# Attention stage of a hybrid decoder step: queries and keys whole in fp32 with two heads in the array's row halves, a values product with queries in partitions, and sample scores four batches at a time

## The chip, the cores and the metric

The kernel runs on one core of a Trainium2 chip. The metric is the device time of one execution in microseconds (us). Engines are named as in the profile: PE is TensorE's matrix multiplication, PEld its weight load, DVE is VectorE, ACT ScalarE, POOL GpSimd, SP SyncE.

## What is computed

One step of a one-layer decoder with 512 prompt tokens and a group of 8 samples of 4 tokens each (32 rows), which share the weights. The two paths read one combined projection:

```python
h = rmsnorm(x, g) * (1 + mods[1]) + mods[0]
q, kc, vc, kv_sel, kv_win, gates, z, xbc, dt = in_proj(h, w_in, g_q, g_k_sel, g_k_win)
# attention: 8 query heads, 2 key-value heads, head size 64
s = jnp.einsum('btgqd,bmgd->btgqm', q, k) * SCALE      # SCALE = 64 ** -0.5
p = masked_softmax(s, mask)
o = jnp.einsum('btgqm,bmgd->btgqd', p, v)
o = gates[:, :, 0] * o_cmp + gates[:, :, 1] * o_sel + gates[:, :, 2] * o_win
# state-space path: causal conv on x/B/C, chunked scan, gate and norm
x = x + mods[2] * (concat(rmsnorm(o), y_ssm) @ w_out)
x = x + mods[5] * hier_moe(rmsnorm(x, g2) * (1 + mods[4]) + mods[3], ...)
```

Attention has three branches: compressed blocks of 32 tokens, selected blocks of 64, and a window of 512. For the prompt the window covers all 512 tokens and at most 8 blocks exist, so its selected and window branches are both causal attention, with different keys and values. The samples have a past of 2048 tokens in paged caches; their selected branch ranks 32 blocks and gathers pages, and their window branch reads a cache of 512 rows.

## The kernel before

Tokens of the prompt lie in four tiles of 128 (`t` = 0 to 3). The program has four stages, each with its own set of PSUM tiles: modulation weights, projections with the prompt's state-space chunks, the attention stage (from `open_psum("pp2", ...)`, L768), and the out projection with the expert part (MoE).

The order of instructions on each engine is not the order of the source alone: a scheduler sets it when the program is built, from data dependencies, buffers and priorities, and it mixes independent pieces. So what stands beside what has to be read from the built order.

In the attention stage the prompt's two causal branches are eight calls `attend(t, br)`, `br` = 1 for the window (`wino` holds keys and values) and 0 for the selected branch (`selo`). Queries `QT` and keys `KT` are kept transposed and in fp32r, a 32-bit form that PE takes in one pass, as a high part and the rest: each head's 64 query columns are split into high and rest over 128 rows (L903 to L915, tile `qhl`), and keys stand twice, once for each half (`k_stack`, L775 to L791, tile `khl`). One head's scores are then two matmuls on 128 rows, and a third adds the causal mask `negm` on the diagonal block (L806 to L813). DVE reduces the row maximum (L815, `amx`), ACT takes the exponential (L817, `psb`), PE transposes it (L820, `pt`), an evacuation (`evac`, L100 on DVE or L102 on ACT) copies it to `ptsb`, and the values product writes `ot` with head columns in partitions, two heads in the two column halves of the array:

```python
mm(ot[64 * i:64 * i + 64, h2 * P:(h2 + 1) * P], src[:, c, P + g * 64:P + (g + 1) * 64],
   pts[i][:, c * P:(c + 1) * P], start=c == 0, stop=c == t)
```

Here the values (64 columns) are stationary and 128 queries move. At the end `ot` is copied (`ots`, L829), transposed back in four transposes (L836), scaled by gate and sum on DVE (L838), and added into `att` on POOL (L841). Score tiles `s` have two buffers of one bank.

The samples' work runs between these calls: `win_half` and `sel_first`/`sel_second` for two halves of four batches. Each transposes gathered keys (`kt<-sm`, L1023), multiplies them by the block-diagonal queries `Qb` (`smo<-kt,Qb`: a 32-column block per batch, 512 columns), and takes a softmax and a values product (`smo<-gsel,kt`). Before that DVE norms and scales the sample rows (L854 to L872) and ranks the blocks (L1201 to L1205). The samples' state-space chain (L1244 to L1348: conv `xcS`, states `hst`, decay `dcS`, sums L1340) and the prompt's compressed attention (L1355 to L1420) are also in this stage. The next stage begins with the transposes of `zy` (L1521), which need the PSUM tiles of the attention stage.

All matmuls are issued by the helper at L92. An fp32 matmul shows as two records of the profile, an fp32r or bf16 one as one.

Of the kernel before, what the change touches and what calls it, by code (L numbers as in the profile page):

```python
# [9 lines left out]
F32 = mybir.dt.float32  # L10
F32R = mybir.dt.float32r
# [39 lines left out]
def hybrid_step(ctx: ExitStack, tc: tile.TileContext, a, o):  # L51
# [501 lines left out]
    V.tensor_scalar_mul(gq8, gq, SCALE)  # L553

# [195 lines left out]

    steps = dict(C=proj_c, z=proj_z, p=ssd_prep, q=proj_q, B=proj_b, e=ssd_end)
# [16 lines left out]
    open_psum("pp2", s=2, pt=2, ot=1, sm=2, smo=1)  # L768
# [3 lines left out]
    QT = p2.tile([P, 8, 512], F32R, name="QT")  # L772
    KT = p2.tile([P, 2, 2, 2, 512], F32R, name="KT")

    def k_stack(src, br):  # L775
        kq = W(p2, [P, NT, P], F32, "t512", 2)
        V.tensor_tensor(kq.rearrange("p t (g d) -> p t g d", d=64),
                        src[:, :, 0:P].rearrange("p t (g d) -> p t g d", d=64),
                        gq8[:, None, None, :].to_broadcast([P, NT, 2, 64]), op=OP.mult)
        kq4 = kq.rearrange("p t (g d) -> p (t g) d", d=64)[:, :, None, :].to_broadcast([P, NT * 2, 2, 64])  # L780
        khl = SLOT([P, 2, NT * 2, 2, 64], F32R, "khl")
        V.tensor_copy(khl[:, 0], kq4)
        V.tensor_sub(khl[:, 1], kq4, khl[:, 0].bitcast(F32))
        for g in range(2):
            for hl in range(2):
                x = khl[:, hl]
                ps = PS("s")
                for t in range(NT):
                    T.transpose(ps[:, t * P:(t + 1) * P],
                                x[:, 2 * t + g].rearrange("p a d -> p (a d)").bitcast(F32), ident)  # L790
                evac(KT[:, br, g, hl, :], ps)  # L791


# [6 lines left out]
    def attend(t, br, first=False):  # L800
# [4 lines left out]
        for h2 in range(4):  # L805
            pts = []  # L806
            for h in (2 * h2, 2 * h2 + 1):
                g = h // 4
                ps = PS("s")
                q = QT[:, h, t * P:(t + 1) * P]  # L810
                mm(ps[:, 0:n], q, KT[:, br, g, 0, 0:n], start=True, stop=False)
                mm(ps[:, 0:n], q, KT[:, br, g, 1, 0:n], start=False, stop=False)
                mm(ps[:, t * P:n], identb, negm, start=False, stop=True)  # L813
                mx = W(p2, [P, 1], F32, "amx", 4)
                V.tensor_reduce(mx, ps[:, 0:n], axis=AX.X, op=OP.max, negate=True)  # L815
                pb = W(p2, [P, 512], F32, "psb", 3)
                S.activation(pb[:, 0:n], ps[:, 0:n], AF.Exp, bias=mx, accum_out=sm[:, h:h + 1])  # L817
# [3 lines left out]
                pts_sb = W(p2, [P, 512], F32, "ptsb", 3)  # L821
                evac(pts_sb[:, 0:n], pt[:, 0:n])
                pts.append(pts_sb)
            g = h2 // 2
            for c in range(t + 1):
                for i in range(2):
                    mm(ot[64 * i:64 * i + 64, h2 * P:(h2 + 1) * P], src[:, c, P + g * 64:P + (g + 1) * 64],
                       pts[i][:, c * P:(c + 1) * P], start=c == 0, stop=c == t)
        ots = W(p2, [P, 512], F32, "psb", 3)  # L829
        evac(ots, ot)  # L830
# [3 lines left out]
        po = PS("s")  # L834
        for h2 in range(4):
            T.transpose(po[:, h2 * P:(h2 + 1) * P], ots[:, h2 * P:(h2 + 1) * P], ident)  # L836
        tmp = att[:, t, :] if first else W(p2, [P, 512], F32, "t512", 2)
        V.tensor_tensor(tmp.rearrange("p (h d) -> p h d", d=64), po.rearrange("p (h d) -> p h d", d=64),  # L838
                        sm[:, :, None].to_broadcast([P, 8, 64]), op=OP.mult)
        if not first:  # L840
            G.tensor_add(att[:, t, :], att[:, t, :], tmp)  # L841
# [61 lines left out]
    for t in range(NT):  # L903
        qn3 = qa[:, t, :].rearrange("p (h d) -> p h d", d=64)
        if t % 2 == 0:
            qhl = SLOT([P, 2, 8, 2, 64], F32R, "qhl")
        q2 = qhl[:, t % 2]
        S.copy(q2[:, :, 0, :], qn3)
        V.tensor_sub(q2[:, :, 1, :], qn3, q2[:, :, 0, :].bitcast(F32))
        for hf in range(2):  # L910
            ps = PS("s")
            for h in range(4):
                T.transpose(ps[:, h * P:(h + 1) * P], q2[:, 4 * hf + h].rearrange("p a d -> p (a d)").bitcast(F32),
                            ident)
            evac(QT[:, 4 * hf:4 * hf + 4, t * P:(t + 1) * P], ps.rearrange("p (h c) -> p h c", c=P))  # L915


    pi = C3([P, 1], I32, "pi3")
    G.iota(pi, pattern=[[0, 1]], base=0, channel_multiplier=1)
    io8 = C3([P, 8], F32, "io8")  # L920
    G.iota(io8, pattern=[[1, 8]], base=0, channel_multiplier=0, allow_small_or_imprecise_dtypes=True)
    ia = C3([P, 1], I32, "ia")
    ib = C3([P, 1], I32, "ib")
    tf = C3([P, 1], F32, "tf")
    gqf = C3([P, 1], F32, "gqf")
    V.tensor_scalar(ia, pi, 2, 3, op0=OP.logical_shift_right, op1=OP.bitwise_and)
    V.tensor_copy(tf, ia)
# [1248 lines left out]
```

## Time and profile before

| | us |
|---|---|
| median of 3 runs | 783.35 (783.32 to 785.89) |
| the profiled execution | 787.62 |
| its span, first to last instruction | 785.9 |
| attention stage, first query transpose to first `zy` transpose | 258.45 to 489.19 |

The profile comes from one execution, the 787.62 one. The span is what the trace shows; 1.7 us lie around it. Durations of matmuls are modelled and overlap their neighbours in a pipeline, so the distance between two starts says more than one duration. A clock of 1.0 is TensorE's upper level, 2.4 GHz, and 0.5 the lower, 1.2 GHz.

### The profile page before, as it was taken

To read this page: it belongs to the slowest core of one execution; us is meant where nothing else is said; L and a number is where in the kernel's file an instruction comes from. 1 tells how busy PE (TensorE), PEld (TensorE's weight loads), DVE (VectorE), ACT (ScalarE), POOL (GpSimd) and SP (SyncE) were. 2 spreads that over 40 slices of the span, in tenths; PEclk is the share of its full clock that TensorE was granted. 3 is DMA by queue.
4 is the path that set the end of the run, shared out by engine and by line. 5 is a ranking of instruction groups with operands and counts; after the bars stand their busy time and mean duration, and the time that the engine had idled before them with its cause. 6 is when DMAs were issued, how large, how long until landed. Compare 5 with 4: busy or idle time off the path is not lost. (4 is left out here: it accounts for less than half of the span.)

```text
span 785.9 us, 14689 instructions
## 1 busy us (share of the span) xinstructions
PE 709.3 (90%) x5565; PEld 511.7 (65%) x5565; DVE 501.2 (64%) x1333; ACT 355.2 (45%) x813; POOL 151.6 (19%) x169
## 2 busy tenths in 40 slices
PE   4999999898999578998989999899668999999993
PEld 3667877676777355665647756687655766767562
DVE  5633692524644767554557555878986888877773
ACT  3423444515233333364434435613433766677661
POOL 1103012121321421010111200020131232233221
PEclk9999999889899879699999889999868999999997
DMA  8964895144559634423445041988767899997311
GB/s 286 355 187 131 289 330 193 58 162 161 214 191 346 253 143 172 149 81 134 164 158 219 2 108 23 360 267 286 290 253 282 270 333 335 334 329 256 86 25 23
DMA packets 67094, 161.86 MB, mean 206 GB/s; under 512 B 19005, under 2 KB 31238, under 8 KB 60622
## 3 DMA queue, kind: packets, MB, share of 16 engines
q1 hardware_dynamic: 56798, 115.54, 42.3%
q0 software_dynamic: 10224, 45.37, 17.5%
q8 instruction: 44, 0.72, 0.4%
q14 instruction: 28, 0.23, 0.1%
HBM read 153.48 MB, written 20.74 MB: 222 GB/s over the span
## 5 line engine op out<-in xcount | busy, mean ns | idle before, releaser
L92 PE MATMUL acc<-wh,hH 128*128 128x512 f32 (+1 forms) x128 | 48.9, 382 | 0.5 <-issue 0.5
L92 PE MATMUL acc<-wl,hH 128*128 128x512 f32 (+1 forms) x128 | 47.3, 370 | 0.0
L92 PE MATMUL acc<-wh,hL 128*128 128x512 f32 (+1 forms) x128 | 47.1, 368 | 0.0
L817 ACT ACTIVATE psb<-s,amx 128x128 f32<-128x128 f32 (+3 forms) x64 | 33.7, 528 | 27.4 <-DVE amx L815 24.3
L92 PE MATMUL acc<-gu,XF 128*128 128x512 f32 x88 | 46.1, 606 | 0.0
L92 PE MATMUL acc<-wh,XH 128*128 128x512 f32 x68 | 44.7, 657 | 0.4 <-ACT XH L1942 0.4
L815 DVE TENSOR_REDUCE amx<-s 128x1 f32<-128x128 f32 (+3 forms) x64 | 30.9, 484 | 17.3 <-PE s L92 17.3
L92 PE MATMUL ps<-wada,scT 128*32 128x128 f32 x768 | 38.0, 301 | 4.1 <-DMA wada<-in_w_ada 3.0
L92 PE MATMUL s<-KT,QT 128*128 128x384 f32 (+3 forms) x128 | 39.3, 392 | 1.3 <-DVE qa L838 0.8
L335 DVE TENSOR_TENSOR wl<-dn,wh 128x512 fp32r<-128x512 f32 x52 | 34.0, 686 | 7.0 <-ACT wh L334 6.9
L92 PEld LDWEIGHTS ps<-wada,scT 128*32 128x32 f32 x768 | 30.6, 122 | 10.3 <-issue 3.6
L1047 POOL DMA_INDIRECT gsel<-in_cache_sel,idx x16 | 20.6, 1289 | 84.3 <-PE smo L92 72.6
L334 ACT CAST wh<-dn 128x512 fp32r<-128x512 f32 x52 | 30.9, 619 | 12.9 <-PE acc L92 11.2
L820 PE MATMUL pt<-ident,psb 128*128 128x128 f32 x160 | 33.3, 308 | 3.3 <-ACT psb L817 3.3
L1991 POOL DMA_INDIRECT out_y_prompt<-yo,gi x13 | 21.4, 1646 | 74.8 <-DVE yo L1985 20.1
L335 DVE TENSOR_TENSOR wl<-gu,wh 128x512 fp32r<-128x512 f32 x44 | 29.5, 685 | 8.4 <-ACT wh L334 7.6
L92 PE MATMUL acc<-wh,HH 128*128 128x512 f32 x68 | 32.3, 478 | 1.6 <-ACT HH L1974 1.2
L334 ACT CAST wh<-gu 128x512 fp32r<-128x512 f32 x44 | 26.1, 619 | 15.8 <-PE acc L92 10.8
L92 PE MATMUL smo<-kt,Qb 128*32 128x512 f32 x80 | 29.6, 614 | 2.3 <-DVE kt L100 2.3
L102 ACT COPY kt<-sm 128x512 f32<-128x512 f32 x32 | 18.5, 584 | 27.6 <-PE sm L1023 24.0
L1985 DVE TENSOR_TENSOR yo<-acc,M 128x512 f32<-128x512 f32 x34 | 23.1, 686 | 11.5 <-PE acc L92 9.1
L92 PE MATMUL acc<-wl,HH 128*128 128x512 f32 x68 | 28.6, 421 | 0.0
(788 smaller groups left out, 1902.9 us busy)
## 6 DMA issues: line engine op xcount, KB each, us to landing
wada<-in_w_ada SPq DMA_DIRECT2D x24, 1024.0 KB
dn<-in_w_down SPq DMA_DIRECT2D x12, 1024.0 KB
gu<-in_w_gate SPq DMA_DIRECT2D x21, 512.0 KB
gu<-in_w_up SPq DMA_DIRECT2D x21, 512.0 KB
gux<-in_w_gate SPq DMA_DIRECT2D x11, 512.0 KB
gux<-in_w_up SPq DMA_DIRECT2D x11, 512.0 KB
wt<-in_cache_win SPq DMA_DIRECT2D x4, 1024.0 KB
wout<-in_w_out SPq DMA_DIRECT2D x4, 1024.0 KB
```

Source lines behind the costliest of these rows:

```text
L92: T.matmul(out, lhsT, rhs, start=start, stop=stop)
L102: S.copy(out, in_)
L334: S.copy(wh[:, 0:n], w)
L335: (eng or V).tensor_sub(wl[:, 0:n], w, wh[:, 0:n].bitcast(F32))
L815: V.tensor_reduce(mx, ps[:, 0:n], axis=AX.X, op=OP.max, negate=True)
L817: S.activation(pb[:, 0:n], ps[:, 0:n], AF.Exp, bias=mx, accum_out=sm[:, h:h + 1])
L820: T.transpose(pt[:, c * P:(c + 1) * P], pb[:, c * P:(c + 1) * P], ident)
L1047: G.indirect_dma_start(out=t.rearrange("p r c -> p (r c)"), out_offset=None, in_=sel_rows, in_offset=bass.IndirectOffsetOnAxis(ap=idx[:, 2 ...
L1985: V.tensor_tensor(yo[:, cols], po, M5[:, cols], op=OP.mult)
L1991: G.indirect_dma_start(out=y_p, out_offset=bass.IndirectOffsetOnAxis(ap=gi, axis=0), in_=yo, in_offset=None, bounds_check=511, oob_is_err= ...
```

## The change

Queries and keys stay whole in fp32. A tile of 128 rows holds one head of each of the two key-value groups (`q` of group 0 in rows 0 to 63, `q` of group 1 in rows 64 to 127), so one transpose serves two heads, the scale goes onto the keys when ACT copies them out (`k_turn`), and the two heads' scores are matmuls on 64 rows each, in the upper and the lower half of the array. They write a score tile of two banks, of which there is one. For t below 2 one reduction covers both heads. The values product has the transposed weights stationary and 64 value columns moving, so `ot` has queries in partitions; the copy and the four transposes at the end are gone, and the sum into `att` is on DVE. `psb` and `ptsb` have four buffers. The sample scores of four batches are issued by `four_scores`, which ties them to each other in the order 3, 0, 1, 2. Constants and masks are made before the projections, under a lower priority; the window cache tiles have a pool of their own, and the first two gathers are issued early. The source order of the calls is other than before. The compressed scores become four matmuls.

```diff
+    def PS2(tag):
+        return psum["pool"].tile([P, 2, 512], F32, name=nm(tag), tag=tag, bufs=psum["tags"][tag])
...
+    gqc = const([P, 1], F32, "gqc")
+    V.tensor_scalar_mul(gqc, gqr, SCALE)
...
-                S.copy(qa[:, t, :], acc[t])
+                S.copy(qa[:, t, :].rearrange("p (q g d) -> p q g d", q=4, g=2),
+                       acc[t].rearrange("p (g q d) -> p q g d", q=4, g=2))
...
+    with tc.high_priority(offset=-2500):
...
+        PB = CS([P, 2, 8], F32, "PB")
...
-    open_psum("pp2", s=2, pt=2, ot=1, sm=2, smo=1)
+    open_psum("pp2", s=1, pt=2, ot=1, sm=2, smo=1)
...
-    QT = p2.tile([P, 8, 512], F32R, name="QT")
-    KT = p2.tile([P, 2, 2, 2, 512], F32R, name="KT")
-
-    def k_stack(src, br):
...
+    QT = p2.tile([P, 4, 512], F32, name="QT")
+    KT = p2.tile([P, 2, 512], F32, name="KT")
+
+    def k_turn(src, br):
+
+        ps = PS("pt")
+        for t in range(NT):
+            T.transpose(ps[:, t * P:(t + 1) * P], src[:, t, 0:P], ident)
+        S.activation(KT[:, br], ps, AF.Copy, scale=gqc)
...
+        for q in range(4):
+            s2 = PS2("s")
+            for g in range(2):
+                gs = slice(64 * g, 64 * g + 64)
+                mm(s2[:, g, 0:n], QT[gs, q, t * P:n], KT[gs, br, 0:n], start=True, stop=False)
+            for g in range(2):
+                mm(s2[:, g, t * P:n], identb, negm, start=False, stop=True)
+            mx = W(p2, [P, 2], F32, "amx", 4)
+            if t < 2:
+                V.tensor_reduce(mx, s2[:, :, 0:n], axis=AX.X, op=OP.max, negate=True)
+            else:
+                for g in range(2):
+                    V.tensor_reduce(mx[:, g:g + 1], s2[:, g, 0:n], axis=AX.X, op=OP.max, negate=True)
+            for g in range(2):
+                h = 4 * g + q
+                pb = W(p2, [P, 512], F32, "psb", 4)
+                S.activation(pb[:, 0:n], s2[:, g, 0:n], AF.Exp, bias=mx[:, g:g + 1], accum_out=sm[:, h:h + 1])
                 pt = PS("pt")
                 for c in range(t + 1):
                     T.transpose(pt[:, c * P:(c + 1) * P], pb[:, c * P:(c + 1) * P], ident)
...
+                for c in range(t + 1):
+                    mm(ot[:, 64 * h:64 * h + 64], pts[:, c * P:(c + 1) * P], src[:, c, P + g * 64:P + (g + 1) * 64],
+                       start=c == 0, stop=c == t)
-        ots = W(p2, [P, 512], F32, "psb", 3)
-        evac(ots, ot)
...
-        po = PS("s")
-        for h2 in range(4):
-            T.transpose(po[:, h2 * P:(h2 + 1) * P], ots[:, h2 * P:(h2 + 1) * P], ident)
...
-            G.tensor_add(att[:, t, :], att[:, t, :], tmp)
+            V.tensor_add(att[:, t, :], att[:, t, :], tmp)
...
+        ps = PS("pt")
+        for q in range(4):
+            T.transpose(ps[:, q * P:(q + 1) * P], qa[:, t, q * P:(q + 1) * P], ident)
+        evac(QT[:, :, t * P:(t + 1) * P], ps.rearrange("p (q c) -> p q c", c=P))
...
+    def four_scores(hb, ps, kts, start=True):
+
+        last = None
+        for b4 in (3, 0, 1, 2):
+            b = 4 * hb + b4
+            i = T.matmul(ps[32 * b4:32 * b4 + 32, :], Qf[:, 32 * b:32 * b + 32], kts[b4], start=start, stop=True).ins
+            if last is not None:
+                tc.add_manual_dep(i, last.name, mybir.DependencyInfo(mybir.DependencyClass.NoSync,
+                                                                     mybir.DependencyReason.DATA), reason="four_scores")
+            last = i
...
-            for b4 in range(4):
-                b = 4 * hb + b4
-                mm(sc[32 * b4:32 * b4 + 32, :], Qf[:, 32 * b:32 * b + 32], kts[b4], start=False, stop=True)
+            four_scores(hb, sc, kts, False)
...
-            w = SLOT([P, 2, 4, 256], name="wt")
+            w = W(p3, [P, 2, 4, 256], F32, "wt", 2)
...
     first0 = sel_first(0, gt00)
+    wt1 = win_load(1)
+    gt10 = gather_half(1, 0)
     attend(0, 1, True)
-    gt01 = gather_half(0, 1)
+    sel_second(0, gt01, *first0)
+    gt11 = gather_half(1, 1)
     attend(1, 1, True)
-    wt1 = win_load(1)
-    sel_second(0, gt01, *first0)
     win_half(1, wt1)
+    first1 = sel_first(1, gt10)
     attend(0, 0)
-    gt10 = gather_half(1, 0)
-    first1 = sel_first(1, gt10)
+    attend(2, 1, True)
+    sel_second(1, gt11, *first1)
...
-    attend(2, 1, True)
     attend(3, 1, True)
...
-    for h in range(8):
-        for j in range(2):
-            mm(pcs, kcT[:, h // 4, j, 112 - 16 * h:240 - 16 * h], QT[:, h, :], start=h == 0 and j == 0,
-               stop=h == 7 and j == 1)
+    for q in range(4):
+        mm(pcs, kcT[:, 112 - 16 * q:240 - 16 * q], QT[:, q, :], start=q == 0, stop=q == 3)
...
-    gt11 = gather_half(1, 1)
     attend(1, 0)
     attend(2, 0)
     attend(3, 0)
-    sel_second(1, gt11, *first1)
```

The built order on PE, at three places. First, sample scores `smo<-kt,Qb` of one group of four in the program before, with transposes of gathered keys (`sm<-ident,gsel`) and pieces of an attend between them:

```order
L92 MATMUL smo_3324<-kt_3301,Qb_2907 32x512
L92 MATMUL ot_3941<-ptsb_4042,selo 64x128
L1023 MATMUL sm_3317<-ident,gsel_3188 128x128 x4
L92 MATMUL smo_3324<-kt_3308,Qb_2907 32x512
L92 MATMUL smo_3324<-kt_3315,Qb_2907 32x512
L1023 MATMUL sm_3332<-ident,gsel_3182 128x128 x4
L836 MATMUL s_4051<-ident,psb_4046 128x128 x4
L92 MATMUL s_4413<-KT,QT 128x384 x2
L92 LDWEIGHTS identb
L92 MATMUL s_4413<-negm,identb 128x128
L92 MATMUL smo_3324<-kt_3322,Qb_2907 32x512
```

A group of four in the changed program:

```order
L1055 MATMUL smo_3274<-kt_3272,Qb_2974 32x512
L1055 MATMUL smo_3274<-kt_3251,Qb_2974 32x512
L1055 MATMUL smo_3274<-kt_3258,Qb_2974 32x512
L1055 MATMUL smo_3274<-kt_3265,Qb_2974 32x512
L1030 MATMUL sm_3289<-ident,gsel_3031 128x128 x4
```

The four now stand in a row everywhere; over the program 27 runs of such scores have become ten.

Second, an attend of the prompt, before (t = 0, window branch; `smo` and `sm` are the samples'):

```order
L820 MATMUL pt_3487<-ident,psb_3485 128x128
L92 MATMUL s_3505<-KT,QT 128x128 x2
L92 LDWEIGHTS identb
L92 MATMUL s_3505<-negm,identb 128x128
L92 MATMUL ot_3426<-ptsb_3475,wino 64x128
L1023 MATMUL sm_3078<-ident,wt_3062 128x128 x4
L92 MATMUL smo_3092<-kt_3069,Qb_2907 32x512
L820 MATMUL pt_3499<-ident,psb_3497 128x128
```

The same in the changed program, where a row of `s<-KT,QT` with x2 is the two heads of a pair:

```order
L95 MATMUL s_3410<-KT,QT 128x128 x2
L95 LDWEIGHTS identb
L95 MATMUL s_3410<-negm,identb 128x128
L95 LDWEIGHTS identb
L95 MATMUL s_3410<-negm,identb 128x128
L95 MATMUL ot_3388<-wino,ptsb_3400 128x64
L95 MATMUL ot_3388<-wino,ptsb_3407 128x64
L889 MATMUL pt_3419<-ident,psb_3417 128x128
L889 MATMUL pt_3426<-ident,psb_3424 128x128
```

Both heads' scores stand together now, then both products, then both transposes, and between rows 995 and 1066 the order holds little else than attend(0,1) and attend(1,1).

Third, the end of the stage: the last rows before the `zy` transposes, in the program before, which are the samples' last values products (`smo<-gsel,kt` and `smo<-selnew`) and the last attend's:

```order
L92 MATMUL ot_5103<-ptsb_5246,selo 64x128
L92 MATMUL smo_5360<-gsel_4814,kt_5389 32x128
L92 MATMUL smo_5360<-gsel_4808,kt_5389 32x128
L92 MATMUL smo_5360<-gsel_4810,kt_5389 32x128
L92 MATMUL smo_5360<-gsel_4812,kt_5389 32x128
L92 MATMUL smo_5360<-gsel_4814,kt_5389 32x128
L92 MATMUL smo_5360<-selnew_2883,snT_5356 32x128 x4
L836 MATMUL s_5261<-ident,psb_5256 128x128 x4
L1521 MATMUL ps_5552<-ident,zy 128x128 x4
```

In the changed program the same place holds the state-space chain of the samples:

```order
L95 MATMUL sm_4474<-xcS_4381 32x32
L95 MATMUL sm_4477<-xcS_4381 32x32
L95 MATMUL sm_4480<-rhs_963,lhS_4481 32x32 x8
L95 MATMUL sm_4493<-ident,yo_4464 32x128 x4
L95 MATMUL sm_4506<-s2k_4400,dcS_4491 32x64 x8
L95 MATMUL sm_4522<-pbs_4519,s2k_4471 128x512
L95 MATMUL sm_4526<-pbs_4519,s2k_4471 128x512
L95 MATMUL sm_4530<-pbs_4519,s2k_4471 128x512
L95 MATMUL sm_4534<-pbs_4519,s2k_4471 128x512
L1514 MATMUL ps_5260<-ident,zy 128x128 x4
```

That chain stood between attends before (its first transposes are row 1478 of 2888); now it is behind all attends and all other sample work.

## Rows read from the trace of the kernel before

**Rows 1.** The page, part 1: busy us, share of the span, instructions.

```profile
PE 709.3 (90%) x5565; PEld 511.7 (65%) x5565; DVE 501.2 (64%) x1333; ACT 355.2 (45%) x813; POOL 151.6 (19%) x169
```

**Rows 2.** TensorE timeline, 258 to 278: start, duration, line, op, records [idle].

```profile
258.45 1.09 PE L913 MATMUL s<-ident,qhl 128*128 128x128 f32 x8
...
268.21 1.12 PE L913 MATMUL s<-ident,qhl 128*128 128x128 f32 x4 [3.19 <-DVE QT L100]
...
276.87 0.44 PE L92 MATMUL s<-KT,QT 128*128 128x128 f32 x2
```

**Rows 3.** Busy time by stretch: length, engines, clock, DMA share, GB/s.

```profile
258.00:492.00 234.00, 213.68 (x1696) 140.57 (x1688) 142.79 (x420) 101.81 (x280) 40.01 (x58) 0.91 0.39 136
258.45:276.87 18.42, 11.22 (x68) 8.09 (x64) 17.04 (x59) 7.75 (x18) 8.77 (x18) 0.81 0.81 300
265.90:272.70 6.80, 4.17 (x16) 3.00 (x16) 6.80 (x23) 1.20 (x3) 3.10 (x1) 0.50 1.00 407
460.00:492.00 32.00, 32.00 (x290) 20.04 (x288) 17.22 (x46) 17.23 (x43) 2.99 (x5) 0.99 0.28 76
520.00:786.00 266.00, 235.56 (x1255) 167.22 (x1254) 206.28 (x483) 142.11 (x276) 64.33 (x47) 0.93 0.72 245
```

**Rows 4.** Groups, 255 to 495: shapes, records, busy us, mean ns, idle before.

```profile
L820 PE MATMUL pt<-ident,psb 128*128 128x128 f32 x160 | 33.3, 308 | 3.3 <-ACT psb L817 3.3
...
L92 PE MATMUL ot<-ptsb,selo 128*64 128x128 f32 x160 | 18.7, 311 | 0.5 <-ACT ptsb L102 0.5
...
L92 PE MATMUL ot<-ptsb,wino 128*64 128x128 f32 x160 | 18.4, 293 | 1.2 <-DVE ptsb L100 0.7 <-ACT ptsb L102 0.5
...
L92 PE MATMUL s<-KT,QT 128*128 128x256 f32 x32 | 7.7, 324 | 0.2
...
L815 DVE TENSOR_REDUCE amx<-s 128x1 f32<-128x256 f32 x16 | 6.7, 419 | 0.9 <-PE s L92 0.9
...
L817 ACT ACTIVATE psb<-s,amx 128x128 f32<-128x128 f32 x16 | 5.9, 367 | 12.1 <-DVE amx L815 12.1
...
L836 PE MATMUL s<-ident,psb 128*128 128x128 f32 x32 | 5.5, 299 | 2.3 <-DVE mx L1008 1.2 <-ACT psb L102 1.1
...
L872 DVE TENSOR_TENSOR s2k<-s2k,gq 32x512 f32<-32x512 f32 x1 | 3.2, 3225 | 0.0
...
L102 ACT CAST QT<-s 128x512 fp32r<-128x512 f32 x5 | 2.9, 575 | 6.0 <-PE s L913 6.0
...
L100 DVE CAST QT<-s 128x512 fp32r<-128x512 f32 x3 | 2.0, 678 | 4.4 <-PE s L913 4.4
```

**Rows 5.** TensorE timeline: sample scores in a run of four, then alone.

```profile
338.30 1.07 PE L92 MATMUL smo<-kt,Qb 128*32 128x512 f32 x8
339.30 0.43 PE L92 MATMUL ot<-ptsb,wino 128*64 128x128 f32 x2
...
362.33 1.05 PE L92 MATMUL smo<-kt,Qb 128*32 128x512 f32 x2
363.31 0.66 PE L1023 MATMUL sm<-ident,gsel 128*128 128x128 f32 x4
```

**Rows 6.** TensorE timeline, 147 to 191: shapes from the prompt's state-space chunks.

```profile
148.37 1.00 PE L92 MATMUL ps<-xt,dec 128*128 128x64 f32 x8
...
152.74 0.77 PE L92 MATMUL ps<-ST,xx 64*128 64x256 f32 x4
...
189.82 0.70 PE L92 MATMUL ps<-ST,xx 64*128 64x256 f32 x2
```

**Rows 7.** Group `ps<-xt,dec`, 95 to 262.

```profile
L92 PE MATMUL ps<-xt,dec 128*128 128x64 f32 x64 | 12.1, 330 | 3.4 <-DVE dec L664 3.4
```

**Rows 8.** TensorE timeline, 415 to 490: the state-space chain's first transposes, then `zy`.

```profile
415.90 0.49 PE L1244 MATMUL sm<-ident,us 32*128 32x32 f32 x5
...
489.19 1.04 PE L1521 MATMUL ps<-ident,zy 128*128 128x128 f32 x8
```

**Rows 9.** Line L1340, the chain's last sums: duration min/median/max, first and last start.

```profile
L1340 DVE TENSOR_TENSOR hst<-hst,sm x4: 687/689/689, 449.7 to 456.1; 128x512 f32<-128x512 f32 x4
```

More of the change, by code (lines that the diff above doesn't have):

```diff
@@ L456, in hybrid_step @@
         SP.dma_start(pti, dram(a["page_table"], 0, [[1, 8], [16, NB], [8, 2]]))
+        gqr = const([P, 1], F32, "gqr")
+        SP.dma_start(gqr, dram(a["g_q"], 0, [[0, 2], [1, 64], [1, 1]]))
         gq, gks, gkw, gkc = [brow(name, 64) for name in ("g_q", "g_k_sel", "g_k_win", "g_k_cmp")]
@@ L820, in attend @@
                     T.transpose(pt[:, c * P:(c + 1) * P], pb[:, c * P:(c + 1) * P], ident)
[L821 to L828, printed above, removed]
-        ots = W(p2, [P, 512], F32, "psb", 3)
-        evac(ots, ot)
+                pts = W(p2, [P, 512], F32, "ptsb", 4)
+                evac(pts[:, 0:n], pt[:, 0:n])
+                for c in range(t + 1):
+                    mm(ot[:, 64 * h:64 * h + 64], pts[:, c * P:(c + 1) * P], src[:, c, P + g * 64:P + (g + 1) * 64],
+                       start=c == 0, stop=c == t)
         V.tensor_scalar_max(sm, sm, TINY)
@@ L833, in attend @@
         V.tensor_mul(sm, sm, sg[:, t, 8 + 8 * br:16 + 8 * br])
-        po = PS("s")
-        for h2 in range(4):
-            T.transpose(po[:, h2 * P:(h2 + 1) * P], ots[:, h2 * P:(h2 + 1) * P], ident)
         tmp = att[:, t, :] if first else W(p2, [P, 512], F32, "t512", 2)
-        V.tensor_tensor(tmp.rearrange("p (h d) -> p h d", d=64), po.rearrange("p (h d) -> p h d", d=64),
+        V.tensor_tensor(tmp.rearrange("p (h d) -> p h d", d=64), ot.rearrange("p (h d) -> p h d", d=64),
                         sm[:, :, None].to_broadcast([P, 8, 64]), op=OP.mult)
         if not first:
-            G.tensor_add(att[:, t, :], att[:, t, :], tmp)
+            V.tensor_add(att[:, t, :], att[:, t, :], tmp)
     p3, close_p3 = pool("p3")
@@ L903, in hybrid_step @@
     for t in range(NT):
[L904 to L915, printed above, removed]
@@ L1116, in win_half @@
         sw = PS("smo")
-        for b4 in range(4):
-            b = 4 * hb + b4
-            mm(sw[32 * b4:32 * b4 + 32, :], Qf[:, 32 * b:32 * b + 32], kts[b4])
+        four_scores(hb, sw, kts)
         sw0 = sw.rearrange("p (i c) -> p i c", c=P)[:, :, 0]
@@ L1130, in win_half @@
         add_rows(hb, po, factor(hb, 2, sm))
-    k_stack(wino, 1)
+    k_turn(wino, 1)
     wt0 = win_load(0)
+    gt00 = gather_half(0, 0)
+    gt01 = gather_half(0, 1)
     win_half(0, wt0)
-    k_stack(selo, 0)
-    gt00 = gather_half(0, 0)
+    k_turn(selo, 0)
     kn = W(p3, [64, NB, P], F32, "pbs", 1)
@@ L1359, in hybrid_step @@
     V.tensor_tensor(k3, k3, gkc[0:16, None, :].to_broadcast([16, 2, 64]), op=OP.mult)
[L1360 to L1362 removed]
+    ps = PS("pt")
+    T.transpose(ps[:, 0:16], kcv[:, 0:P], ident[0:16, 0:16])
+    kcT = W(p2, [P, 240], F32, "kcT", 1)
+    V.memset(kcT, 0.0)
     for g in range(2):
[L1364 to L1372 removed]
+        gs = slice(64 * g, 64 * g + 64)
+        V.tensor_scalar_mul(kcT[gs, 112 + 64 * g:128 + 64 * g], ps[gs, 0:16], gqc[gs])
+    ps = PS("pt")
     mm(ps[:, 0:P], rep.rearrange("p h c -> p (h c)"), kcv[:, P:256])
[L1374 to L1375 removed]
     vblk = W(p2, [P, 2, 4, 64], F32, "vblk", 1)
```

180 lines of the change are left out of this document (71 added, 109 removed).

## The prediction

> **What bounds the kernel now.** I read the page's busy shares first, then busy time by stretch, then TensorE's timeline, then the groups of instructions of the attention stage. The page puts PE at 90% of the span [rows 1]. The stage that the change rewrites, from the first query transpose at 258.45 [rows 2] to the first `zy` transpose at 489.19 [rows 8], lasts 230.7 us. Over 258 to 492 PE is busy 213.7 of 234 us; DVE is busy 142.8 and ACT 101.8 [rows 3]. So the stage is bound by PE, with 20.3 us of waits. Its last 32 us have none: PE is busy 32.00 of 32.00 [rows 3]. From 520 to the end PE is busy 235.6 of 266 and the DMA engines 0.72 [rows 3], so I let the start of that part decide the end one for one: a microsecond won before 489.19 is won at the end.
>
> One place is not PE's: the preparation of queries and keys, 258.45 to the first scores at 276.87 [rows 2]. There DVE is busy 17.0 of 18.4 us and PE 11.2 [rows 3], with the clock at half (0.50) from 265.9 to 272.7 [rows 3], a stretch in which PE stood 3.19 us for a DVE evacuation before 268.21 [rows 2].
>
> **The change part by part.** All terms are against the profiled execution: 787.6 us, a span of 785.9 and 1.7 around it. It is 4.3 us above the median of the runs shown, 783.35, so I take 4.3 off at the end.
>
> Preparation. The hi/lo copies, the doubled heads and 40 of 64 transposes go. What is left is 24 transposes in six groups of four. Eight in a row took 1.09 us [rows 2], four take 0.66 [rows 5], and the evacuation of four 0.58 on ACT or 0.68 on DVE [rows 4], with two tiles in turn: six groups by some 0.7 and the first one's lead make about 5 us in place of 18.4. Term: -13.4. DVE's sample work that shared the 18.4 us stays, and is charged below.
>
> Sample scores. Each batch uses a quarter of the array's columns. One matmul alone (two records) took from 362.33 to 363.31, 0.98 us; four in a row (eight records) from 338.30 to 339.30, 1.00 us [rows 5]. So a run of one costs as much as a run of four. The order has 40 such matmuls in 27 runs before and in ten runs of four after: 17 runs by 0.98 are gone. Term: -17. The order fixes this, and the least it can be is 0, if PE then waits for the fourth `kt` of each group.
>
> Scores of the prompt. Two fp32r passes over doubled heads become one fp32 matmul (two records) on 64 rows, two heads in the two row halves. The trace has that shape once: `ps<-ST,xx`, two heads (four records, 256 columns) in 0.77 us where one head alone (two records) takes 0.70 [rows 6]. So halves do run side by side: 0.77 for the pair, where now a head of 256 columns has two of the 32 records of 7.7 us, 0.48, and two heads 0.96 of busy time that overlaps its neighbours [rows 4]. Other widths aren't shown in that shape, so I take no change for the scores themselves. For the alternation of row halves and whole array, 32 times, no row gives a price of its own; I take 4 us, a good tenth of a microsecond each time. The ends: serial halves would cost the pair another 0.70, for all widths about +24 (32 pairs by some 0.75); and -6 if every pair gains the 0.2 of this one.
>
> Values product. Before: 320 records, two heads side by side in column halves, 18.7 + 18.4 = 37.1 us [rows 4]. After: 320 records with 128 stationary columns and only 64 moving ones. The trace has exactly this shape in `ps<-xt,dec`: eight in a row took 1.00 us, 0.125 each, while the whole group of 64 averages 12.1 / 64 = 0.189 [rows 6, 7]. So 40 to 60.5 us, +3 to +23. At t=3 eight records of a head, often sixteen of two, stand in a row, so I go by the run of eight: +4. The Trainium skill speaks against this edit: its page "TensorEngine Tiling (Array Packing)", section Performance Considerations, advises for a moving size of 64 or less to swap the operands and tile the columns, which is what the old form does. By an estimate from that page's factor of up to two, undoing it would cost up to +37 in place of +4. The run of eight at 0.125 does not bear that out; the group's 0.189 goes part of the way, and is a rival below.
>
> What the product's new layout saves: 32 transposes of `ots` at the end of each attend (5.5 us and 2.3 of waits) [rows 4] and eight copies on ACT and DVE. Term: -7.8. The sum into `att` leaves POOL for DVE, four adds of an evacuation's 0.68; off PE's path, since DVE is busy 142.8 of 234 us [rows 3]. The `pt` transposes (33.3 us, [rows 4]) now come in neighbouring pairs of heads instead of alternating with products: between 0 and -6, I take -3. The masks and constants made ahead of the projections, and the earlier gathers and window loads, I cost at nothing: the projections' matmuls hide the first, and the second wait for no one sooner than now; without cover they are some 3 us of DVE.
>
> Sum of PE's own work and the waits that go with it: -13.4 - 17 + 4 + 4 - 7.8 - 3 = -33.
>
> New waits. Three, all read from the order.
> (a) The score tile is now one two-bank tile where there were two. The next pair's scores stand behind both exponentials of this pair. For a pair of 128 columns that is a reduction of 0.42 and two exponentials of 0.37 [rows 4] plus hand-overs, with the scores themselves about 1.95 us a round, against some 1.1 us of PE work (scores, masks, two transposes, two products; both are estimates): 0.85 a pair. Where other work fills in it costs nothing; attend(0,1) runs alone, 4 pairs, 3.4 us. From 0 to 14 if no long attend hides it either.
> (b) DVE's sample preparation and its ranking of blocks (one step alone 3.2 us, [rows 4]) now lie beside attend(1,1) and attend(2,1) alone, and the compressed attention's chain stands with little beside it. Between 0 and the DVE time of the preparation stretch, 17.0 us [rows 3], which holds most of the same sample work; I take 15.
> (c) The sample's state-space chain. Before, it lay between attends from 415.90 to the last `hst` sum at 456.1 + 0.69, 40.9 us [rows 8, 9]. After, it is the last thing of the stage on PE: behind the last values product of the samples, 22 rows, nothing of the prompt beside them, and the `zy` transposes behind it. On ACT its tanh also stands behind four casts of a `wout` tile, whose load waits for a gather's buffer. Of the 40.9 us much was queueing behind attends; I take half, 20, of which 10 is its own matmuls (an estimate: `Cb` and the `hst` transposes and sums are some 60 short ones): 10 idle, between 0 and 30.
> Together 28. Of the 20.3 us of waits before, 7.2 (of the preparation, 18.4 less PE's busy time there, [rows 3]) and 2.3 (before the `ots` transposes) are already in the terms above; the other 10.8 lie in the same places as the new ones and are replaced. Net +17.6.
>
> Sum: -33 + 17.6 = -15.4. Profiled: about 772. Median: 783.35 - 15.4 = 768.
>
> **The rivals.**
> The waits stay hidden: the 28 us shrink to the 10.8 of before and PE's whole saving comes through, -33: 750. For it: PE was kept full for 32 us at the end of the present stage [rows 3] by just such a mixture. Against it: the order has runs of attend alone.
> The values product is bound by its weight load, at the 0.189 of the whole `ps<-xt,dec` group [rows 7]: 19 us more than I took, -15.4 + 19 = +4 less the waits it fills, about +1: 784, no change. It speaks for this that products of one and two records are the rule at t=0 and t=1; against it that half of all records are in runs of eight.
> Slower: the state-space tail. If the chain, alone, still takes its 40.9 us, and PE, which waits there over and over, shows half clock as around the 3.19 us wait [rows 2, 3], its idle is 30 in place of 10 and its own matmuls of 10 cost 20: +30, so +15: 798. It decides from 16 us beyond my 10 on.
> The row halves do not run side by side in this stream: +24, so +9: 792. Against it is the one measured pair [rows 6].
>
> **How the numbers follow.** Forecast 768 with its own range 760 to 777: 0.50. Waits hidden, 750: 0.20. Product load-bound, 784: 0.10. Tail, 798: 0.13. Serial halves, 792: 0.07. What this kernel's measurement can tell from no change is about 0.5%, 4 us, so 779 to 787 is the same. Faster: 0.50 + 0.20 + 0.03 of the third (some of it below 779) = 0.73; same 0.08; slower 0.19. The range, 749 to 790, leaves out the far ends of the first and third rival.
>
> **What would show it.** Right: first scores near 263 to 264; `smo<-kt,Qb` in ten runs of about 1.0 us; scores of two heads starting within 0.1 us of each other; values products 0.125 us or less a record; no `po` transposes; PE idle of some 10 us, in many short waits, in the last 30 us before `zy`, and that start at 472 to 476. Wrong: `zy` before 465 (the waits were hidden) or after 485 (tail or product), a half clock in most of the stage, or a wait in the MoE part that gives the gain back because expert weights arrive no earlier than now.

## The result and the profile after

The changed kernel takes 789.78 us (median of 20 runs, 786.48 to 797.72) against 786.37 for the kernel before (20 runs, 779.47 to 790.93): ratio 1.006, interval 1.0036 to 1.0085. Some executions fall into a slower state, and ratios here compare the fast ones alone, so 1.006 is not the quotient of the two medians. The kernel is slower by about half a per cent; 768 was forecast, 15.4 less than the 783.35 that was known of the kernel before. Of the cases put on record, the one whose place and mechanism came is the rival of the state-space tail, which had a chance of 0.13; its size, 798, did not come.

The profiled execution has a span of 788.2 us. Busy time by stretch, of the changed kernel, with the columns of [rows 3]:

```profile
258.00:492.00 234.00, 202.56 (x1604) 143.72 (x1605) 136.52 (x389) 99.91 (x280) 25.91 (x40) 0.83 0.38 142
440.50:491.00 50.50, 35.30 (x216) 25.54 (x216) 29.77 (x105) 13.93 (x35) 6.44 (x18) 0.54 0.25 88
460.00:492.00 32.00, 27.35 (x120) 20.09 (x121) 17.71 (x56) 6.30 (x15) 6.44 (x18) 0.50 0.21 77
520.00:788.00 268.00, 236.54 (x1264) 168.22 (x1262) 206.58 (x483) 141.90 (x276) 63.83 (x47) 0.93 0.72 240
```

Over 258 to 492 PE is busy 202.6 us where it was 213.7 [rows 3]: the work did shrink. But the granted clock is 0.83 in place of 0.91, and the last 32 us, which were full at a clock of 0.99, now run at 0.50 with 4.6 us of waits. The part from 520 on is nearly the same in all columns.

The groups that the terms of the sum were about, of the changed kernel, 255 to 495 (columns of [rows 4]):

```profile
L889 PE MATMUL pt<-ident,psb 128*128 128x128 f32 x160 | 29.9, 306 | 6.9 <-ACT psb L886 6.4 <-DVE qa L1412 0.3
L95 PE MATMUL ot<-wino,ptsb 128*128 128x64 f32 x160 | 25.6, 311 | 0.2 <-ACT ptsb L105 0.2
...
L95 PE MATMUL ot<-selo,ptsb 128*128 128x64 f32 x160 | 20.6, 274 | 0.0
...
L1055 PE MATMUL smo<-kt,Qb 128*32 128x512 f32 x80 | 11.5, 650 | 1.2 <-ACT kt L105 1.2
```

The sample scores of the kernel before, on its page:

```profile
L92 PE MATMUL smo<-kt,Qb 128*32 128x512 f32 x80 | 29.6, 614 | 2.3 <-DVE kt L100 2.3
```

They fell from 29.6 us to 11.5. The values product rose from 37.1 [rows 4] to 46.2, and `pt` fell from 33.3 [rows 4] to 29.9.

TensorE's timeline of the changed kernel, first the start of the stage, and one pair of long score matmuls:

```profile
260.89 1.09 PE L967 MATMUL pt<-ident,qa 128*128 128x128 f32 x8
...
265.59 0.49 PE L95 MATMUL s<-KT,QT 64*128 64x128 f32 x4 [0.29 <-ACT KT L857]
...
309.56 0.92 PE L95 MATMUL s<-KT,QT 64*128 64x384 f32 x4
310.41 0.29 PE L95 MATMUL s<-negm,identb 128*128 128x128 bf16 x2
```

Preparation takes 4.7 us (260.89 to 265.59), not 18.4 [rows 2]. The stage itself begins 2.4 us later than before. Then the end:

```profile
440.48 1.07 PE L1055 MATMUL smo<-kt,Qb 128*32 128x512 f32 x8 [0.32 <-ACT kt L105]
446.12 0.40 PE L1022 MATMUL sm<-ident,sn 128*32 128x128 f32 x1 [4.58 <-ACT sn L1020]
...
449.68 3.64 PE L95 MATMUL smo<-gsel,kt 128*32 128x128 f32 x64
...
461.40 1.23 PE L1269 MATMUL sm<-ident,xcS 128*32 128x128 f32 x5 [6.75 <-DVE xcS L1266]
...
483.08 7.19 PE L95 MATMUL sm<-pbs,s2k 32*128 32x512 f32 x8 [0.51 <-DVE atS L1336]
491.04 1.97 PE L1514 MATMUL ps<-ident,zy 128*128 128x128 f32 x8 [0.78 <-DVE hst L1348]
```

The last scores of the samples end 441.5, with all attends done. From there to `zy` at 491.04 only the last sample part and the state-space chain are left, 49.5 us. PE waits 15.2 of the 50.5 us from 440.5 on, and its 35.3 busy us run at a clock of 0.54, which is some 18 to 19 us of work at the upper level, by an estimate from that clock.

ACT in the same place (changed kernel): an out-projection cast waits for its load, and the chain's tanh stands behind it.

```profile
458.43 2.18 ACT L1685 CAST wH<-wout 128x512 fp32r<-128x512 f32 x4 [9.58 <-DMA wout<-in_w_out]
460.51 0.36 ACT L1264 ACTIVATE tmS<-xcS 128x192 f32<-128x192 f32 x1
```

### The profile page after: what moved, and what is told of

It reads as the page before. It is cut to its first block, busy times and chain, and to the rows that moved or that the text cites. A ratio compares the mean times of both kernels' runs of the same rounds, so it can differ in the third digit from the quotient of the medians.

```text
span 788.2 us, 14431 instructions
## 1 busy us (share of the span) xinstructions
PE 702.8 (89%) x5484; PEld 518.8 (66%) x5484; DVE 490.8 (62%) x1302; ACT 346.7 (44%) x799; POOL 143.5 (18%) x165
## 5 line engine op out<-in xcount | busy, mean ns | idle before, releaser
L889 PE MATMUL pt<-ident,psb 128*128 128x128 f32 x160 | 29.9, 306 | 6.9 <-ACT psb L886 6.4
L337 ACT CAST wh<-dn 128x512 fp32r<-128x512 f32 x52 | 30.8, 619 | 10.7 <-PE acc L95 8.8
L1065 POOL DMA_INDIRECT gsel<-in_cache_sel,idx x16 | 15.3, 956 | 95.2 <-PE smo L95 87.7
L95 PE MATMUL s<-KT,QT 64*128 64x384 f32 (+3 forms) x128 | 29.9, 539 | 0.3 <-ACT KT L857 0.3
L105 ACT COPY kt<-sm 128x512 f32<-128x512 f32 x32 | 18.5, 588 | 25.6 <-PE sm L1030 18.9
L889 PEld LDWEIGHTS pt<-ident,psb 128*128 128x128 f32 x160 | 19.5, 152 | 14.8 <-ACT psb L886 12.8
L95 PEld LDWEIGHTS acc<-wh,hH 128*128 128x128 f32 x128 | 24.1, 188 | 7.2 <-issue 3.2
```

Of the source, the lines that this page charges most:

```text
L95: T.matmul(out, lhsT, rhs, start=start, stop=stop)
L105: S.copy(out, in_)
L337: S.copy(wh[:, 0:n], w)
L889: T.transpose(pt[:, c * P:(c + 1) * P], pb[:, c * P:(c + 1) * P], ident)
L1065: G.indirect_dma_start(out=t.rearrange("p r c -> p (r c)"), out_offset=None, in_=sel_rows, in_offset=bass.IndirectOffsetOnAxis(ap=idx[:, 2 ...
```

## The experiments

All times are medians beside runs of the kernel before on the same chip; a ratio is to that kernel, with its 95% interval. The changed kernel's 1.006 is the number to hold them against. Profiles are best compared from the stage's own start: in the changed kernel and its variants, none of which touches the source ahead of the stage, the first query transpose lies anywhere from 255.3 to 261.7.

**e1_end.** One call moved:

```diff
     attend(2, 1, True)
-    sel_second(1, gt11, *first1)
     hst = SLOT([P, NB, 4, 64], name="hst")
...
     attend(3, 0)
+    sel_second(1, gt11, *first1)
```

> The changed kernel, with one call moved: the last sample part, sel_second(1), is called after attend(3,0) and so behind the state-space chain of the samples, not ahead of it; in the built order the chain now stands beside the second half of attend(3,0) and is followed by that sample part. Theory (tail): the changed kernel's 49 us from 441.5 to 491.0 in which PE has only that chain and its last sample part are the loss; with other work beside the chain the two long waits (4.6 and 6.8 us) and most of the half clock go, zy starts near 475 and the kernel takes about 775 us (770 to 780). Rival (load of wout): ACT stands behind the late load of an out-projection weight wherever the chain is; about 786. Rival (attention itself is slow, single score tile): no change, 789 to 791.

Measured: 772.18 us, ratio 0.9864 (0.9813 to 0.9914). The time is the one that the tail's theory gave: one call's place is worth some 15 us. The end of the stage, TensorE's timeline of e1_end:

```profile
448.11 7.19 PE L95 MATMUL sm<-pbs,s2k 32*128 32x512 f32 x8
...
459.84 1.06 PE L1055 MATMUL smo<-kt,Qb 128*32 128x512 f32 x8
...
468.10 0.28 PE L1022 MATMUL sm<-ident,sn 128*32 128x128 f32 x1 [3.54 <-ACT sn L1020]
...
473.17 1.10 PE L1514 MATMUL ps<-ident,zy 128*128 128x128 f32 x8
```

`zy` starts at 473.17, against 491.04; 4.8 of these 17.9 us lie ahead of the stage, which begins at 256.05 against 260.89. The chain no longer waits alone: its conv gap of 6.75 us is filled by attend(3,0), and over the stage PE waits 18.3 us where it waited 30.6. The clock did not do what was expected, though. Busy time by stretch, of e1_end:

```profile
440.00:450.00 10.00, 10.00 (x59) 7.32 (x59) 8.83 (x24) 3.48 (x10) 2.63 (x12) 0.50 0.05 15
450.00:460.00 10.00, 9.74 (x31) 4.84 (x33) 8.04 (x32) 2.08 (x5) 0.00 (x0) 0.58 0.32 74
```

PE is busy nearly without a break, and the clock is still 0.50 while the chain's small matmuls run. So what the moved call gives back is waits; the half clock, which the theory expected to go as well, stayed.

**x_fill.** Transposes that nothing reads, placed where PE waits:

```diff
+    fl = PS("pt")
+    with tc.high_priority(offset=-5000):
+        for n in range(100):
+            i = T.transpose(fl[:, 0:P], ident, ident).ins
+            tc.add_manual_dep(i, (marks[-1] if n < 40 else conv_in).name, ...)
```

(`marks[-1]` is the last sample score, `conv_in` the last conv transpose.)

> The changed kernel with 100 transposes of a constant added, which nothing reads, behind the last sample scores (40) and behind the conv transposes of the chain (60): 10.9 us of PE work at the full clock, put where PE waits. Theory (tail, half clock): PE's clock stays at its upper level behind 446, the chain's matmuls take half as long, and in spite of the added work the kernel is faster: about 779 us (776 to 784). Rival (the chain's waits on DVE, ACT and loads alone set the tail): no gain, 790, and up to 10 slower where the added work stands ahead of the chain: 790 to 800.

Measured: 781.14 us, ratio 0.9984 (0.9952 to 1.0015). With 10.9 us of useless work added, the kernel is some 6 us faster than the changed kernel's 1.006. But only half of the theory held. The fillers kept the clock up as long as they ran, and it fell at 462.5, behind them. TensorE's timeline, then the stretches, of x_fill:

```profile
437.24 1.06 PE L1057 MATMUL smo<-kt,Qb 128*32 128x512 f32 x8 [0.32 <-ACT kt L105]
438.23 4.58 PE L1422 MATMUL pt<-ident 128*128 128x128 f32 x40
...
448.50 6.01 PE L1422 MATMUL pt<-ident 128*128 128x128 f32 x53
...
481.35 1.97 PE L1523 MATMUL ps<-ident,zy 128*128 128x128 f32 x8
```

```profile
450.00:460.00 10.00, 7.66 (x66) 6.77 (x65) 5.96 (x16) 5.10 (x10) 0.00 (x0) 1.00 1.03 390
460.00:470.00 10.00, 9.40 (x70) 8.87 (x69) 3.13 (x7) 1.95 (x5) 4.04 (x4) 0.62 0.05 18
470.00:480.00 10.00, 9.29 (x31) 5.03 (x30) 8.53 (x35) 0.72 (x2) 2.40 (x15) 0.50 0.01 2
```

From 460 on PE is busy 94% and 93% and the clock still falls to 0.62 and 0.50. From the last sample scores to `zy` this kernel takes 44.1 us (437.24 to 481.35), the changed one 50.6 (440.48 to 491.04). The wait from these scores to the next `sn` transpose is as long in both (5.64 us from start to start, to 442.88 here), and the one ahead of `xcS` is no shorter (7.2 us against 6.75). So the 6.4 us come from matmuls that ran at the upper level: the clock is a real part of the tail.

**x_wh.** The casts of the second out-projection half behind the chain on ACT:

```diff
-        S.copy(wH[:, k, :], w1(k))
+        ci = S.copy(wH[:, k, :], w1(k)).ins
+        tc.add_manual_dep(ci, ssd_act.name, ...)   # ssd_act: the chain's last ACT step
```

> The changed kernel with the eight casts of the second half of the out-projection weight put behind the state-space chain on ACT, so that the tanh of the chain does not stand behind casts that wait 9.6 us for a load. Theory (tail): the conv sum is ready 3.0 us before ACT is, so 3 us go: about 787. Rival (load of wout sets the tail): most of the 9.6 us goes, about 781, since the clock would not fall either.

Measured: 783.26 us, ratio 0.9974 (0.9939 to 1.0008), some 7 us below the changed kernel: between the two. TensorE's timeline of x_wh:

```profile
454.00 1.23 PE L1269 MATMUL sm<-ident,xcS 128*32 128x128 f32 x5 [4.17 <-DVE xcS L1266]
...
481.34 1.97 PE L1514 MATMUL ps<-ident,zy 128*128 128x128 f32 x8 [0.78 <-DVE hst L1348]
```

The conv gap is 4.17 in place of 6.75, so 2.6 us are the cast's directly, as the tail's theory had it. Another 2.3 us are in the chain behind it, 27.3 us from 454.00 to `zy` where the changed kernel takes 29.6 from 461.40; its clock is 1.00 from 457.5 to 460.9, where the changed kernel's chain has 0.50 throughout. The rest I can't tell from the spread of runs. In e1_wh, where the chain is not alone, the same edit gives nothing that can be told (below), so the late load is not the cause but one more wait in the tail.

**e2_f1.** The chain's source moved ahead of `sel_first(1)`, and its state load ahead of the last gathers:

```diff
+    hst = SLOT([P, NB, 4, 64], name="hst")
+    SP.dma_start(hst, ...)
     gt11 = gather_half(1, 1)
     attend(1, 1, True)
     win_half(1, wt1)
+    # the chain
     first1 = sel_first(1, gt10)
```

> The changed kernel with the chain's source moved ahead of sel_first(1) and its state load ahead of the last gathers; in the built order the chain lies among attend(2,0) and attend(3,0), and the stage ends with the second half of the samples' selected and window branches (about 130 rows of transposes and scores) alone. Theory (tail): PE has work at the end, the clock holds, zy near 472: about 772 us (766 to 780). Rival (attention itself is slow): 788 to 791. Rival (whatever stands alone at the end costs as much): the samples' part alone waits for evacuations, 783 to 790.

Measured: 793.18 us, ratio 1.0109 (1.0049 to 1.0168). The theory as put fell: it isn't enough that the chain is covered. The last rival came, and beyond its number: now the samples' second half stands alone at the end, and it waits for its gathers. Parts of the chain, though covered, ran at the lower clock here too: around its last sums the clock is 0.50 from 428.7 to 445.8, with PE busy all of these 17.1 us. TensorE's timeline of e2_f1:

```profile
475.47 1.94 PE L1030 MATMUL sm<-ident,gsel 128*128 128x128 f32 x8 [7.64 <-DMA gsel<-in_cache_sel,idx]
...
483.19 1.03 PE L1030 MATMUL sm<-ident,gsel 128*128 128x128 f32 x4 [2.56 <-ACT kt L105]
...
495.17 1.09 PE L1514 MATMUL ps<-ident,zy 128*128 128x128 f32 x8
```

**b_four.** The kernel before with `four_scores` in the two places of the samples' scores (the selected branch's, which the diff above shows, and the window branch's, which it leaves out), and nothing else.

> The kernel before with one edit: the sample scores of four batches are tied together as in the change. Theory (four matmuls side by side cost what one costs, 17 runs of 0.98 us go, the stage is bound by PE): 17 us less, 767 to 773 against 784 before. Rival (PE then waits for the fourth key tile of each group, or the order around it is worse): 0 to 6 less.

Measured: 776.35 us, ratio 0.9895 (0.9839 to 0.995): 8 us, between theory and rival; the interval (4 to 13 us) stops short of 17. The group itself fell as it should. The group and the stage, first query transpose to `zy`, in b_four:

```profile
L1048 PE MATMUL smo<-kt,Qb 128*32 128x512 f32 x80 | 10.7, 605 | 0.5 <-ACT kt L102 0.5
```

```profile
258.69:473.92 215.23, 191.84 (x1644) 134.95 (x1641) 142.54 (x419) 99.73 (x276) 38.12 (x54) 0.90 0.41 144
```

The stage is 15.5 us shorter than the 230.7 of before, with PE 18.6 us less busy than the 210.4 it was there and 3 us more of waits. In this profile the part behind `zy` is longer: 300.5 us to the end of the span, against 296.7. Over the profiles of all these kernels that part takes 294.5 to 300.5, so this one profile doesn't tell a cost from chance.

**e1_nofour.** e1_end with the four scores issued as before, untied.

> e1_end without the tie between the four sample scores. Theory: the runs split again into some 25, each about 1 us: 12 to 15 us slower than e1_end, 785. Rival (waits hide it now): the same as e1_end, 772.

Measured: 796.34 us, ratio 1.0143 (1.0098 to 1.0188): 22 us slower than e1_end, more than the 12 to 15 expected. Its stage, 259.04 to 497.87, is 21.7 us longer than e1_end's, with PE 19.8 us busier. In e1_nofour the group is back at its old size:

```profile
L95 PE MATMUL smo<-kt,Qb 128*32 128x512 f32 x80 | 29.8, 611 | 0.0
```

So four adjacent scores are the largest gain in the change, and without them the rest of it, in its best order, is slower than the kernel before.

**e1_oldot.** e1_end with the old values product:

```diff
-                    mm(ot[:, 64 * h:64 * h + 64], pts[:, c * P:(c + 1) * P], src[...], ...)
+                    mm(ot[64 * g:64 * g + 64, q * P:(q + 1) * P], src[...],
+                       pair[g][:, c * P:(c + 1) * P], ...)
+        ots = W(p2, [P, 512], F32, "psb", 4)
+        evac(ots, ot)
+        po = PS("pt")
+        for q in range(4):
+            T.transpose(po[:, q * P:(q + 1) * P], ots[:, q * P:(q + 1) * P], ident)
```

> e1_end with the values product as before (values stationary, two heads in column halves, a copy and four transposes at the end of each attend); everything else stays. Theory (the new product costs 4 us more on PE and saves 7.8): the old one is about 4 us slower, 776. Rival (new product bound by its weight load, 60 us): the old one is about 11 us faster, 761.

Measured: 780.2 us, ratio 0.9934 (0.99 to 0.9969), some 5 us slower than e1_end's 0.9864, though their intervals meet at 0.99. The product and its transposes in e1_oldot:

```profile
L95 PE MATMUL ot<-ptsb,wino 128*64 128x128 f32 x160 | 18.1, 327 | 1.7 <-DVE ptsb L103 1.6
L95 PE MATMUL ot<-ptsb,selo 128*64 128x128 f32 x160 | 18.0, 296 | 0.0
...
L905 PE MATMUL pt<-ident,psb 128*128 128x128 f32 x32 | 5.5, 298 | 1.1 <-ACT psb L105 1.1
```

The old product is 12 us shorter on PE than e1_end's (25.5 + 22.7 = 48.2), yet the kernel isn't faster: the load-bound rival, 761, is excluded. Over the stage (258.95 to 480.92) PE is busy 191.1 us where e1_end's is busy 198.9, transposes of `ots` included, but it waits 30.8 us where e1_end waits 18.3. The clock differs as well: 0.88 over the stage, against 0.85.

**e1_long.** e1_end with the window branch called as t = 3, 2, 1, 0 (`attend(3, 1)` and `attend(2, 1)` in the places of t = 0 and 1, `attend(0, 0)` behind `attend(0, 1)`).

> e1_end with the long attends of the window branch called first (t = 3, 2, 1, 0) instead of t = 0 and 1, so that PE has more work per round of reduction and exponential while DVE prepares the samples. Theory (the first 40 us of the stage, at 0.63 of the clock with 4 to 5 us of waits, pay for the single score tile and DVE): the clock holds there and 8 to 12 us go: about 762. Rival (DVE sets the pace in either order): 770 to 774.

Measured: 781.62 us, ratio 0.9965 (0.9927 to 1.0003): a miss, slower than e1_end. The clock of the first 40 us did rise, from 0.63 to 0.79 (258 to 299 in both), but it fell in other places (0.59 from 440 to 460), and over the whole stage it is 0.86, where e1_end has 0.85. So longer attends at the start moved the lower clock rather than removing it. 5.6 us of the difference between the two profiles lie ahead of the stage.

**e1_wh and e1_pbs2.** e1_end with the edit of x_wh; and e1_end with `"pbs", 2` in place of `"pbs", 1` in all five places of that tile.

> Both orders together: e1_end with the casts of the second half of the out-projection weight behind the chain on ACT. Theory (tail): in e1_end the chain lies beside attend(3,0) and its tanh is no longer late by much, so 0 to 3 us less than e1_end, 769 to 772 against 784 before. Rival (load of wout decides): 6 us less, as in x_wh, 766.

> e1_end with two buffers in place of one for the samples' weights tile (pbs), which the conv state of the chain shares with the sample parts. Theory (the place of the chain in the order is what counts, and the order is nearly that of e1_end): 770 to 774. Rival (the wait for that buffer sets when the chain starts): 5 us or more less, 767 or below.

Measured: 772.21 us, ratio 0.9838 (0.9779 to 0.9896), and 771.74 us, ratio 0.9842 (0.978 to 0.9903). Neither can be told from e1_end; both rivals fall. All three beat both kernels: the one before by some 11 to 13 us, the changed one by 15 to 17.

## Why the prediction was wrong

- **The step that failed is the clock of PE, which the sum puts at nothing**, above all in term (c) of the new waits, the state-space chain at the end of the stage: its matmuls were priced at the upper level (10 us), and only its idle time was added. The balance below shows what came in its place. Stretches at the lower level are taken at half of their busy time, an estimate from the eight `zy` transposes, which take 1.97 us at the lower level (491.04 in the changed kernel) and 1.10 at the upper (473.17 in e1_end). First the whole stage, of the kernel before, the changed one and e1_end:

```profile
258.45:489.19 230.74, 210.42 (x1644) 137.80 (x1641) 141.89 (x419) 99.82 (x275) 38.28 (x54) 0.90 0.38 134
260.89:491.04 230.15, 199.52 (x1563) 141.58 (x1559) 136.52 (x389) 99.91 (x280) 24.25 (x38) 0.83 0.37 139
256.05:473.17 217.12, 198.87 (x1564) 140.16 (x1560) 134.71 (x387) 98.03 (x276) 23.40 (x36) 0.85 0.39 140
```

Then stretches at the lower level: all of the changed kernel; of the kernel before those that are not in [rows 3] or in the last section, the last two with its chain; and the two long ones of e1_end, which has three more of 3.4 us:

```profile
267.10:297.90 30.80, 28.61 (x124) 20.37 (x124) 20.27 (x63) 12.10 (x48) 3.34 (x1) 0.50 0.46 182
366.10:369.50 3.40, 3.40 (x16) 1.51 (x15) 2.23 (x6) 0.59 (x1) 0.17 (x1) 0.50 1.00 424
444.60:491.04 46.44, 34.26 (x208) 25.41 (x208) 27.12 (x95) 10.30 (x26) 6.44 (x18) 0.50 0.26 93
...
279.50:289.80 10.30, 8.21 (x43) 6.98 (x43) 7.13 (x20) 4.17 (x16) 3.05 (x2) 0.50 0.34 117
433.10:440.00 6.90, 6.90 (x33) 5.48 (x32) 3.15 (x8) 2.81 (x8) 4.04 (x4) 0.51 0.02 4
453.60:460.40 6.80, 6.80 (x27) 4.65 (x27) 2.90 (x11) 1.17 (x2) 0.00 (x0) 0.50 0.40 84
...
263.90:294.60 30.70, 28.59 (x127) 21.13 (x127) 20.55 (x63) 12.39 (x48) 3.34 (x1) 0.50 0.45 175
434.60:458.50 23.90, 23.77 (x102) 16.54 (x103) 17.52 (x56) 6.98 (x19) 5.85 (x15) 0.50 0.10 25
```

| us of the stage | before | forecast | changed | e1_end |
|---|---|---|---|---|
| PE's work at the upper level | 190.6 | 167.1 | 166.4 | 167.6 |
| what the lower clock adds | 19.8 | 19.8 | 33.1 | 31.3 |
| waits of PE | 20.3 | 28.4 | 30.6 | 18.3 |
| together | 230.7 | 215.3 | 230.2 | 217.1 |

The forecast's column is its own sum: 33 us less, of which 9.5 are waits, 28.4 us of waits in all, and a clock left as it was. The work came as forecast and the waits nearly so. The clock added 13 us that no term had, 10 of them at the end: half of 34.3 busy us there, against half of 13.7 in the two stretches of before. With 2 us more of waits and the stage's start 2.4 us later, that makes the 17 us by which `zy` is late.
- What e1_end shows is therefore the other part of the tail, its waits. Moving one call takes 12 us of waits out and leaves the clock's part at 31 us. That its `zy`, at 473.17, meets what the forecast needed, 473.8 (489.19 less 15.4), is luck: fewer waits than forecast stand against more time at the lower clock, and the stage began early. The lower clock's own part in the tail is shown by x_fill, for 6 of the changed kernel's 17 us; the other 11 rest on the estimate.
- The rival of the tail had the place and the half clock right. Its idle time was not: it took 30 us for the chain, where the whole end has 15.2. So it came to +15 for the median, and +3.4 was measured. Its chance was too low as well: the order showed the chain alone, and the trace of before showed the clock at the lower level twice in the stretch where the chain lay between attends, at 433.1 to 440 and 453.6 to 460.4. PE's share is full there, and the sum went by the share and not by the clock.
- Right: preparation (4.7 us against 5 forecast); the `pt` transposes (3.4 us less, 3 forecast); scores of two heads side by side (0.85 us for a pair of 384 columns, 309.56 to 310.41); sample scores in ten runs (29.6 to 11.5 us); the `po` transposes gone; the rest of the program from `zy` on unchanged (297.2 us to the end of the span, against 296.7), so that the end moved with `zy`. The rival of serial halves is excluded by the pair of 0.85. The 4 us for the alternation of row halves and whole array were not measured on their own.
- Mis-sized: the values product cost +9 (46.2 against 37.1), not +4: 0.144 us a record, less than a third of the way from the forecast's 0.125 to the load-bound rival's 0.189. Part of the 46.2 is the lower clock in attend(0,1) and attend(1,1), whose group is the dearer one (25.6 against 20.6); at the upper level, by the same estimate, the rise is still some 7 to 8 us. The Trainium skill's advice in "TensorEngine Tiling (Array Packing)", section Performance Considerations, to swap the operands here, agrees with the product's own rows (36.1 us in e1_oldot). For the kernel it didn't decide: PE is busy 7.8 us less in e1_oldot than in e1_end, and the kernel is no faster, since PE waits 12.6 us more. That the copy and the transposes behind the old product make these waits was not shown.
- Sized right on PE, less sure in time: four scores at -17. Untying them costs e1_end 19.8 busy us and 22 us in time; tying them takes 18.6 busy us off the kernel before and 15.5 us off its stage, but only 8 (4 to 13) off its median. Why the median gained less there stays open.
- Since b_four alone reaches 0.9895 and e1_end 0.9864, with intervals that overlap, all the other edits together can't be told from nothing in time, in their best order.

## What to carry to other kernels

Price a step that is moved to where nothing stands beside it with its waits and with its matmuls at the clock that the trace shows for such matmuls; read the granted clock of the stretch where they lie now, not only PE's share. Split a stage into work at the upper level, time added by the lower clock and waits, and see which of the three an experiment moved: a time that meets the forecast can be made up otherwise than the forecast was. What the last rows of a stage are decides as much as how much work it has: before counting savings, look at which dependency chain the new order leaves alone at the end, and try the order with one call moved. Put independent matmuls that each fill a part of the array next to each other in the order, since a scheduler that doesn't know they run side by side will scatter them.

## What was not expected of the hardware

TensorE's clock was at its lower level in stretches in which PE never stood still: in e1_end from 440 to 450, PE busy 10.00 of 10 us, and in the kernel before for 6.8 us from 453.6, PE busy 6.80. Both lie in or right behind the chain's narrow matmuls (32 rows, or 8 to 64 columns). In x_fill the clock was 1.00 as long as whole-array transposes filled part of the waits (450 to 460, PE busy 7.66 of 10), and 0.62 and then 0.50 behind them, with PE busier than before. The narrow matmuls are not the only such place: in the kernel before, 317.1 to 330.7 ran at 0.50 with PE busy 13.60 of 13.60, in an attend of t = 0 behind some short waits. So a full busy share is no sign of the upper clock. Nor do the chain's matmuls alone settle it: in e1_oldot they lie between attends too, from 425.6 to 457.4, but beside the old values product, and the clock is 1.00 there but for 3.4 us; in e1_end, beside the new product, it falls at 434.6, in the middle of the chain, and stays at 0.50 to 458.5. What the narrow matmuls, the product and the waits ahead of them each do was not separated. A stretch of the kernel before, then two of e1_oldot:

```profile
317.10:330.70 13.60, 13.60 (x56) 8.77 (x55) 7.57 (x23) 5.16 (x20) 1.45 (x2) 0.50 0.38 124
```

```profile
425.60:439.20 13.60, 13.45 (x110) 10.49 (x111) 9.04 (x17) 7.22 (x20) 0.00 (x0) 1.00 0.45 160
442.60:457.40 14.80, 14.77 (x122) 8.66 (x121) 11.38 (x32) 4.46 (x11) 3.04 (x13) 1.00 0.00 1
```
